# Two PSUM tiles for the transposes of attention's weights, and products in the order of the blocks

## The chip, the cores and the metric

The kernel runs on one core of a Trainium2 chip. The metric is the device time of one execution in microseconds. Three runs of the kernel before took 2699.07, 2689.06 and 2688.96 us, with a median of 2689.06 us.

## The reference

The reference is a backbone of two layers over 512 latent tokens and 256 context tokens. Each layer projects its input into four token mixers: a bidirectional RWKV-7 scan (A), a convolution module (B), windowed grouped-query attention with a sink logit (C) and multi-head latent attention, MLA (D). Their outputs are gated, projected and summed, and an output projection adds them to the stream. The change touches C and D, where softmax weights meet the values:

```
# C, per block of 128 queries and kv head (4 query heads share one kv head)
o = (jnp.einsum('bnhgqk,bnkhd->bnqhgd', (e_lat * inv).astype(v.dtype), vb)
     + jnp.einsum('bnhgqc,bchd->bnqhgd', (e_ctx * inv).astype(v.dtype), v_c))
# D, per head
p = jax.nn.softmax(s, axis=-1).astype(v.dtype)
return jnp.einsum('bhqk,bkhd->bqhd', p, v)
```

## The kernel before

All activations lie with channels on partitions. Projections are made of matmuls of 128 x 128 weights and 512 or 256 tokens. Each is done three times over on split operands (high by high, high by low, low by high; lines 289 to 291, in `mm3`), and `dense` sums them in a PSUM tile named `d`.

A layer runs in stages: RWKV, then `window` (C), then `mla` (D), then `merge`. The program is written in that order, but a scheduler lays each engine's instructions out ahead of time. It fills TensorE's places in `window` and `mla` with products of `merge` that are ready: gate projections (`hxh`, `hxl`) and branch projections (`uh`, `ul`). These are called fillers below. What is not used up as a filler runs in `merge` itself. Every engine works through its list strictly in order, so a place in the list is fixed before the run.

Attention works in units. A unit of `window` is a block of 128 queries with one kv head, thus four query heads; it has 4 or 5 blocks of 128 keys, or 2 for context queries. A unit of `mla` is one head with all its queries: 6 blocks of keys and 512 queries in the latent part, and 2 blocks and 256 queries in the context part, which layer 0 alone has. For each row of a unit TensorE makes scores in a PSUM tile `S`, VectorE takes the maximum (L1019), ScalarE the exponential (L1025), and VectorE normalises (L1032). The weights lie in an SBUF tile `P` (named `aP` in `window`, `mP` in `mla`) with queries on partitions.

`weighted_values` (L1041) then turns them round. For each block of keys, TensorE transposes the 4 (or 2) pieces of 128 x 128 into the PSUM tile `T` (L1050). `pt_copy` copies `T` back over `P`, by turns on ScalarE (L1037) and VectorE (L1039). Then a matmul for each block multiplies with the values (L1054) and sums in the PSUM tile `E`. A block with an even number writes partitions 0 to 63 of `E`, one with an odd number partitions 64 to 127, so that each half of `E` has its own sum. `halves` (L1060, L1061) adds the two and so empties `E`. Both pools hold one tile: the transposes of a block wait until the copy of the block before is done. The products run from the last block to the first, so that the first product waits for the copy that is made last.

Inside `weighted_values`, TensorE's transposes and products keep the written order among themselves (`manual_schedule`), while the scheduler may still put other work between any two of them. The readout of a unit is placed behind the scores of the next. `T` also serves `conv_norm` and, in layer 0, `ada_later`, which makes the modulation of the next layer in small steps (L379, L389) from weights that come by DMA. Nothing else uses `E` in these two stages.

Of the kernel before, what the change touches and what calls it, by code (L numbers as in the profile page):

```python
# [215 lines left out]
class Net:  # L216
# [821 lines left out]
        else:  # L1038
            self.nc.vector.tensor_copy(out, in_)  # L1039

    def weighted_values(self, P, values, acc):  # L1041


        nc = self.nc
        nk, nb = P.shape[1:3]
        with self.tc.manual_schedule(engines={mybir.EngineType.PE}):
            for x in range(nk):
                pt = self.pT([128, nb, 128])
                for i in range(nb):
                    nc.tensor.transpose(pt[:, i], P[:, x, i], self.c("ident"))  # L1050
                self.pt_copy(P[:, x], pt)
            for n, x in enumerate(reversed(range(nk))):
                half = slice(64 * (x % 2), 64 * (x % 2) + 64)
                nc.tensor.matmul(acc[half], lhsT=values(x), rhs=P[:, x].rearrange("p i q -> p (i q)"),  # L1054
                                 start=n < 2, stop=n >= nk - 2)

    def halves(self, pool, out, acc, tag):

# [60 lines left out]
    def window(self, l, ap, nxt):  # L1119
# [8 lines left out]
        vt = ap.tile([128, 6, 128], F32, tag="avt", name=self.n("avt"), bufs=1)  # L1128
# [7 lines left out]
        for kv in range(2):  # L1136
            rows = slice(64 * kv, 64 * kv + 64)
# [30 lines left out]

        def readout(P, kblocks, kv, st, dst):
            rows = slice(64 * kv, 64 * kv + 64)  # L1170
            acc = self.pE([128, 512])
            self.weighted_values(P, lambda x: vt[:, kblocks[x], rows], acc)
            for _ in range(ASTEP * len(kblocks)):
                next(ada, None)
            self.halves(ap, st[rows].rearrange("p a b -> p (a b)"), acc, "aOh")
            if kv:
                nc.sync.dma_start(dst, st)

        for seg in full[::-1]:
            s0, s1 = seg  # L1180
            lat = s0 > 0
            qs = self.aq if lat else self.window_queries(s0, s1)
            nb = (s1 - s0) // 128
            for b in range(nb):
                lo, hi = (max(0, b - 1), min(nb, b + 2)) if lat else (0, 0)
                kblocks = [0, 1] + [2 + kb for kb in range(lo, hi)]
                nk = len(kblocks)
                st = ap.tile([128, 4, 128], F32, tag="aO", name=self.n("aO"), bufs=2)
                for kv in range(2):
                    P = ap.tile([128, 5, 4, 128], F32, tag="aP", name=self.n("aP"), bufs=2)[:, :nk]  # L1190
                    qt = stack(qs[:, :, 128 * b:128 * b + 128], kv)
                    self.softmax(ap, [(lambda i=i: scores(qt[:, 128 * i:128 * i + 128], kv, b, lo, hi, nb, lat),
                                       P[:, :, i]) for i in range(4)], WA_SCALE,
                                 (self.pm("sink", 4 * kv, 4), sk8[:, 4 * kv:4 * kv + 4]))
                    units += 1
                    if units >= CONV_AT:
                        next(conv, None)
                    if pending:
                        readout(*pending.pop())
                    pending.append((P, kblocks, kv, st, self.y[2][:, :, s0 + 128 * b:s0 + 128 * b + 128]))  # L1200
        readout(*pending.pop())
        for rest in (conv, ada):
            for _ in rest:
# [12 lines left out]
    def mla(self, l, ap):  # L1216
# [39 lines left out]
        for s0, s1 in both:  # L1256
            x = ck[:, s0:s1]
# [4 lines left out]
        vt = ap.tile([128, 6, 512], F32, tag="mvt", name=self.n("mvt"), bufs=1)  # L1262
# [21 lines left out]
        def readout(P, h, s0, s1):  # L1284
            n = s1 - s0
            rows = slice(64 * (h % 2), 64 * (h % 2) + 64)
            acc = self.pE([128, n])
            self.weighted_values(P, lambda kb: vt[:, kb, 64 * h:64 * h + 64], acc)
            st = ap.tile([128, n], F32, tag="mO", name=self.n("mO"), bufs=1)
            self.halves(ap, st[rows], acc, "mOh")  # L1290
            nc.sync.dma_start(self.y[3][rows, h // 2, s0:s1], st[rows])

        for s0, s1 in full[::-1]:
            n = s1 - s0
            lat = s0 > 0
            nb = n // 128
            ksegs = both if lat else (SEG_C,)
            nk = 6 if lat else 2
            qn = [self.hilo(ap, x, f"mq{i}") for i, x in enumerate(normed(
                [load(f"dq{i}", s0, s1, f"mq{'hl'[i]}") for i in range(2)], "qn"))]  # L1300
            for hp in range(4):
# [3 lines left out]
                for hh in range(2):  # L1305
                    h = 2 * hp + hh
# [30 lines left out]
                    P = ap.tile([128, 6, 4, 128], F32, tag="mP", name=self.n("mP"), bufs=2)  # L1337
                    P = P.rearrange("p k i q -> p (k i q)")[:, :nk * n].rearrange("p (k i q) -> p k i q", i=nb, q=128)
                    for b in range(nb):
                        self.softmax(ap, [(lambda: scores(b), P[:, :, b])], MLA_SCALE)  # L1340
                        if b == nb - 2 and pending:
                            readout(*pending.pop())
                    pending.append((P, h, s0, s1))
        readout(*pending.pop())


# [215 lines left out]
```

## Time and profile before

| | |
|---|---|
| median of three runs | 2689.06 us |
| the profiled execution | 2689.9 us |
| its span, from first to last instruction | 2688.1 us |
| TensorE matmul busy | 2498.9 us (93% of the span) |
| VectorE busy | 1900.9 us (71%) |
| ScalarE busy | 1294.8 us (48%) |
| GpSimd busy | 612.1 us (23%) |

In the profile PE is TensorE's matmuls, PEld its weight loads, DVE VectorE and ACT ScalarE. L1050 is a line of the kernel. The recorded end of a matmul is modelled and overlaps the next one. What a matmul costs TensorE is therefore read from its start to the start of the next, not from its duration. A product in plain float32 (L1054) is two matmul records, so that "x12" on that line is six products. In the profiled execution `window` lies at 805 to 1001 us in layer 0 and at 2203 to 2334 us in layer 1, and the units of `mla` at 1117 to 1325 us and at 2400 to 2554 us.

### The profile page before, as it was taken

The page shows a single profiled execution, that of the slowest core. Times are in us where ns is not written, and L with a number is a line of the kernel's source. Part 1 is how long each engine was busy: PE and PEld are TensorE (multiplying, and loading weights), DVE is VectorE, ACT ScalarE, POOL GpSimd, SP SyncE. Part 2 cuts the span into 40 slices and gives each one's busy share as a digit, 9 for nine tenths or more (in the row PEclk, how much of TensorE's full clock was granted, in tenths as well). Part 3 has the DMA queues.
Part 4 walks back from the last instruction along what each step waited for, and adds up shares of the span by engine and source line. Part 5 has one row for each costly group of instructions (what it writes and reads, how often), then busy time and mean ns, then how long its engine had stood idle before and what let it go on. Part 6 is the DMA issues. An engine that isn't in the chain of part 4 may idle for free. (4 is left out here: it accounts for less than half of the span.)

```text
span 2688.1 us, 48510 instructions
## 1 busy us (share of the span) xinstructions
PE 2498.9 (93%) x18622; PEld 1918.6 (71%) x18622; DVE 1900.9 (71%) x3644; ACT 1294.8 (48%) x2723; POOL 612.1 (23%) x644
## 2 busy tenths in 40 slices
PE   7989899898998998999999998897989899999998
PEld 5777777676886676776788876676667666666677
DVE  5788989987527564677633678887777947577835
ACT  5625474554334453445422463554565346555434
POOL 1232222222220111100132013322232421221140
PEclk9999989998999999999999999898999989999999
DMA  6321222223243346112322532223232432331233
GB/s 235 120 91 51 87 73 92 75 77 105 93 136 103 114 141 194 52 36 66 96 81 83 179 105 94 92 72 112 66 108 65 129 109 75 110 102 34 88 123 122
DMA packets 171031, 267.79 MB, mean 100 GB/s; under 512 B 18480, under 2 KB 69552, under 8 KB 170800
## 3 DMA queue, kind: packets, MB, share of 16 engines
q1 hardware_dynamic: 169520, 263.12, 31.1%
q8 instruction: 146, 2.39, 0.4%
q10 hardware_dynamic: 1280, 1.57, 0.2%
q14 instruction: 85, 0.70, 0.1%
HBM read 209.70 MB, written 54.92 MB: 98 GB/s over the span
## 5 line engine op out<-in xcount | busy, mean ns | idle before, releaser
L283 POOL TENSOR_TENSOR wl<-raw,wh 128x512 fp32r<-128x512 f32 x374 | 511.0, 1367 | 1513.1 <-ACT wh L282 1311.1
L289 PE MATMUL d<-hxh,wh 128*128 128x512 f32 (+1 forms) x1936 | 718.0, 371 | 22.8 <-DVE stg L927 12.6
L290 PE MATMUL d<-hxl,wh 128*128 128x512 f32 (+1 forms) x1936 | 717.7, 371 | 0.0
L291 PE MATMUL d<-hxh,wl 128*128 128x512 f32 (+1 forms) x1936 | 713.1, 368 | 0.0
L282 ACT CAST wh<-raw 128x512 fp32r<-128x512 f32 x420 | 259.4, 619 | 518.7 <-PE d L290 339.8
L289 PEld LDWEIGHTS d<-hxh,wh 128*128 128x128 f32 x1936 | 374.3, 193 | 78.2 <-DVE stg L927 10.3
L291 PEld LDWEIGHTS d<-hxh,wl 128*128 128x128 f32 x1936 | 374.1, 193 | 52.2 <-issue 1.6
L290 PEld LDWEIGHTS d<-hxl,wh 128*128 128x128 f32 x1936 | 375.0, 194 | 50.6 <-issue 1.8
L971 DVE SCALAR_TENSOR_TENSOR cacc<-cu,par,cacc 128x512 f32<-128x512 f32 (+1 forms) x360 | 282.0, 783 | 4.0
L289 PE MATMUL d<-uh,wh 128*128 128x512 f32 (+1 forms) x384 | 141.5, 371 | 10.7 <-ACT gt L1376 5.8
L1019 DVE TENSOR_REDUCE st<-S 128x1 f32<-128x768 f32 (+3 forms) x160 | 119.7, 763 | 33.4 <-PE S L1165 15.3
L290 PE MATMUL d<-ul,wh 128*128 128x512 f32 (+1 forms) x384 | 140.5, 367 | 0.2 <-DVE ul L1368 0.2
L291 PE MATMUL d<-uh,wl 128*128 128x512 f32 (+1 forms) x384 | 139.8, 365 | 0.0
L1383 DVE SCALAR_TENSOR_TENSOR gt<-gt,d 128x256 f32<-128x256 f32 (+1 forms) x72 | 42.8, 595 | 126.2 <-PE d L291 124.2
L721 DVE TENSOR_TENSOR Xt<-B,X 128x31 f32<-128x31 f32 (+15 forms) x248 | 107.1, 432 | 5.4 <-POOL X L716 2.0
L723 DVE TENSOR_TENSOR X<-X,Xt 128x31 f32<-128x31 f32 (+15 forms) x248 | 101.3, 409 | 3.1
L1025 ACT ACTIVATE mP<-S,st 128x768 f32<-128x768 f32 (+1 forms) x80 | 65.0, 814 | 68.8 <-DVE st L1021 64.1
L711 ACT COPY AT<-G 32x128 f32<-32x128 f32 x192 | 79.3, 413 | 26.7 <-DVE G L693 24.2
L289 PEld LDWEIGHTS d<-uh,wh 128*128 128x128 f32 x384 | 73.2, 191 | 24.5 <-ACT gt L1376 7.3
L688 PE MATMUL A<-KR,KB 64*128 64x128 f32 (+1 forms) x768 | 79.8, 292 | 7.5 <-DVE G L693 5.3
L843 POOL TENSOR_TENSOR MD<-M,Dl 128x128 f32<-128x128 f32 x80 | 42.4, 529 | 181.2 <-DVE M L845 157.9
L290 PEld LDWEIGHTS d<-ul,wh 128*128 128x128 f32 x384 | 73.3, 191 | 11.3 <-DVE ul L1368 1.5
(325 smaller groups left out, 4830.9 us busy)
## 6 DMA issues: line engine op xcount, KB each, us to landing
raw<-in_w_in SPq DMA_DIRECT2D x316, 256.0 KB, 2.7
raw<-in_w_br SPq DMA_DIRECT2D x64, 256.0 KB, 2.7
ada<-in_ada_slim SPq DMA_DIRECT2D x64, 256.0 KB, 3.3
raw<-in_w_out SPq DMA_DIRECT2D x40, 256.0 KB, 2.8
ada<-in_ada SPq DMA_DIRECT2D x32, 256.0 KB, 5.2
spz<-stg SPq DMA_DIRECT2D x32, 256.0 KB, 2.3
kvx<-wa SPq DMA_DIRECT2D x24, 256.0 KB, 3.4
yl<-y SPq DMA_DIRECT2D x16, 384.0 KB, 3.6
```

Of the source, the lines that this page charges most:

```text
L282: nc.scalar.copy(hi, raw)
L283: self.low_engine.tensor_tensor(out=lo, in0=raw, in1=hi.bitcast(F32), op=ALU.subtract)
L289: mm(ps, lhsT=wh, rhs=xh, start=first, stop=False)
L290: mm(ps, lhsT=wh, rhs=xl, start=False, stop=False)
L291: mm(ps, lhsT=wl, rhs=xh, start=False, stop=last)
L688: nc.tensor.matmul(pss[j][:, i, d, :w], lhsT=KB[rows, d, cl + i].rearrange("p a b -> p (a b)"), rhs=KR[rows, cl + i, 0:w // 64, d, :], sta ...
L711: S.copy(AT[b, :, 4 * x:4 * x + 4].rearrange("p t q -> p q t"), G.rearrange("p j i d t -> p (j i) d t")[b, :, d, 32 * h:32 * h + 32])
L721: V.tensor_tensor(out=tv, in0=B[:, t, 0:t].unsqueeze(2).to_broadcast([128, t, w]), in1=X[:, t:t + 1, t:32].to_broadcast([128, t, w]), op=A ...
L723: V.tensor_tensor(out=X[:, 0:t, t:32], in0=X[:, 0:t, t:32], in1=tv, op=ALU.subtract)
L971: V.scalar_tensor_tensor(out=acc, in0=u[:, k:n + k], scalar=w, in1=acc, op0=ALU.mult, op1=ALU.add)
L1019: V.tensor_reduce(out=m[:, i:i + 1], in_=ps, axis=AX.X, op=ALU.max)
L1025: S.activation(P, ps.rearrange("p (k c) -> p k c", c=128), AF.Exp, bias=nm[:, i:i + 1], scale=scale, accum_out=tot[:, i:i + 1])
```

## The change

`weighted_values` makes its own accumulator and returns it. The transposes of a block go to `T` or to a tile of the pool `E` by turns, so that the last block is always in `T` and the one before it in `E`. The accumulator is the next tile of `E`, so that it waits for the copy of the last block but one. The products run from the first block to the last.

```
-    def weighted_values(self, P, values, acc):
+    def weighted_values(self, P, values):
...
             for x in range(nk):
-                pt = self.pT([128, nb, 128])
+                pt = (self.pT if (nk - x) % 2 else self.pE)([128, nb, 128])
                 for i in range(nb):
                     nc.tensor.transpose(pt[:, i], P[:, x, i], self.c("ident"))
                 self.pt_copy(P[:, x], pt)
-            for n, x in enumerate(reversed(range(nk))):
+            acc = self.pE([128, nb * 128])
+            for x in range(nk):
                 half = slice(64 * (x % 2), 64 * (x % 2) + 64)
                 nc.tensor.matmul(acc[half], lhsT=values(x), rhs=P[:, x].rearrange("p i q -> p (i q)"),
-                                 start=n < 2, stop=n >= nk - 2)
+                                 start=x < 2, stop=x >= nk - 2)
+        return acc
...
         def readout(P, kblocks, kv, st, dst):
             rows = slice(64 * kv, 64 * kv + 64)
-            acc = self.pE([128, 512])
-            self.weighted_values(P, lambda x: vt[:, kblocks[x], rows], acc)
+            acc = self.weighted_values(P, lambda x: vt[:, kblocks[x], rows])
...
         def readout(P, h, s0, s1):
             n = s1 - s0
             rows = slice(64 * (h % 2), 64 * (h % 2) + 64)
-            acc = self.pE([128, n])
-            self.weighted_values(P, lambda kb: vt[:, kb, 64 * h:64 * h + 64], acc)
+            acc = self.weighted_values(P, lambda kb: vt[:, kb, 64 * h:64 * h + 64])
```

In the changed kernel the transposes stand on L1051 and the products on L1056; other lines below them move by 3 at most. The scheduler lays out every engine's list anew, and it moves instructions at two kinds of places on TensorE.

The first place is the first unit of `window` with 5 blocks in layer 0, on TensorE. `T` and `E` are the PSUM tiles, `aP` the weights, `avt` the values, `d` a filler, `S` scores. Before, with the first block, the last two and the products:

```order
L1050 MATMUL T_9363<-cst,aP_9130 128x128 x4
L290 MATMUL d_12770<-hxl_405,wh_12765 128x256
...
L1050 MATMUL T_9381<-cst,aP_9130 128x128 x4
L289 MATMUL d_12795<-hxh_402,wh_12759 128x512
L290 MATMUL d_12795<-hxl_403,wh_12759 128x512
L291 MATMUL d_12795<-hxh_402,wl_12760 128x512
L289 MATMUL d_12795<-hxh_404,wh_12765 128x512
L1050 MATMUL T_9387<-cst,aP_9130 128x128 x4
L290 MATMUL d_12795<-hxl_405,wh_12765 128x512
L291 MATMUL d_12795<-hxh_404,wl_12766 128x512
L289 MATMUL d_12795<-hxh_406,wh_12765 128x512
L290 MATMUL d_12795<-hxl_407,wh_12765 128x512
L1054 MATMUL E_9360<-aP_9130,avt_8913 64x512 x5
```

The same unit in the changed kernel, whole:

```order
L1051 MATMUL T_9362<-cst,aP_9130 128x128 x4
L1051 MATMUL E_9368<-cst,aP_9130 128x128 x4
L1051 MATMUL T_9374<-cst,aP_9130 128x128 x4
L1163 MATMUL S_9486<-akh_7822,aqs_9469 128x256
L1164 MATMUL S_9486<-akl_8924,aqs_9469 128x256
L1163 MATMUL S_9486<-akh_7822,aqs_9469 128x384
L1051 MATMUL E_9380<-cst,aP_9130 128x128 x4
L1164 MATMUL S_9486<-akl_8924,aqs_9469 128x384
...
L1051 MATMUL T_9386<-cst,aP_9130 128x128 x4
L1056 MATMUL E_9392<-aP_9130,avt_8913 64x512 x5
```

The fillers between the blocks have moved out of the unit; the five products still stand together, directly behind the last transposes.

The second place is the third latent unit of `mla` in layer 0, on TensorE; `mP` are its weights, `mvt` the values, `ck` and `mku` the operands of the keys' projection for the next head. Before:

```order
L289 MATMUL d_14077<-uh_13480,wh_14059 128x512
L290 MATMUL d_14077<-ul_13481,wh_14059 128x512
L291 MATMUL d_14077<-uh_13480,wl_14060 128x512
L1054 MATMUL E_11470<-mP_11305,mvt_10994 64x512 x6
L1312 MATMUL S_11542<-ck_10969,mku_11540 64x512
```

The same unit in the changed kernel:

```order
L1051 MATMUL T_11502<-cst,mP_11305 128x128 x4
L1056 MATMUL E_11508<-mP_11305,mvt_10994 64x512 x5
L289 MATMUL S_11458<-mKh_11031,mqh_11426 128x512
L290 MATMUL S_11458<-mKl_11032,mqh_11426 128x512
L291 MATMUL S_11458<-mKh_11031,mql_11427 128x512
L289 MATMUL S_11458<-mKh_11031,mqh_11426 128x256
L290 MATMUL S_11458<-mKl_11032,mqh_11426 128x256
L291 MATMUL S_11458<-mKh_11031,mql_11427 128x256
L1056 MATMUL E_11508<-mP_11305,mvt_10994 64x512
L289 MATMUL S_11522<-mKh_11031,mqh_11426 128x512
```

Six products in one group have become a group of five, six score matmuls, and one product by itself. The same happens in 14 of the 16 latent units of `mla`; a fifteenth goes from groups of 4 and 2 to groups of 3, 2 and 1. In 7 of the 8 context units, and in 2 of the 4 context units of `window`, a group of two becomes two products apart.

## Rows read from the trace of the kernel before

**Rows 1.** Busy time by stretch: length, then PE, PEld, DVE, ACT, POOL, PEclk, DMA.
```profile
805.00:1001.00 196.00, 182.93 (x1601) 132.60 (x1599) 131.49 (x308) 98.45 (x225) 23.84 (x18) 0.97 0.39 117
1117.00:1325.00 208.00, 204.77 (x1132) 145.29 (x1131) 156.97 (x321) 107.11 (x233) 24.25 (x18) 1.00 0.18 50
2203.00:2334.00 131.00, 118.27 (x623) 81.71 (x622) 95.55 (x190) 73.91 (x152) 25.04 (x18) 0.96 0.26 81
2400.00:2554.00 154.00, 149.72 (x750) 100.90 (x748) 123.53 (x220) 75.03 (x143) 25.55 (x19) 1.00 0.21 61
```

**Rows 2.** TensorE's waits, 805 to 1001 us: total us, times, longest.
```profile
PE T L1050 <- DVE aP L1039: 2.5, 2, 2.1
...
PE E L1054 <- DVE aP L1039: 1.4, 1, 1.4
...
PE E L1054 <- ACT aP L1037: 0.7, 1, 0.7
```

**Rows 3.** TensorE's waits, 2203 to 2334 us.
```profile
PE E L1054 <- DVE aP L1039: 2.0, 2, 1.4
...
PE T L1050 <- ACT aP L1037: 1.6, 1, 1.6
PE T L1050 <- DVE aP L1039: 1.3, 2, 0.8
```

**Rows 4.** TensorE's waits, 2400 to 2554 us.
```profile
PE T L1050 <- ACT mP L1037: 0.7, 1, 0.7
```

**Rows 5.** Timeline, layer 1's `window`: start us, us, engine, line, operation [idle before].
```profile
2318.25 0.60 PE L1050 MATMUL T<-cst,aP 128*128 128x128 f32 x4
2318.93 0.68 DVE L1039 COPY aP<-T 128x512 f32<-128x512 f32 x1
...
2319.66 0.66 PE L1050 MATMUL T<-cst,aP 128*128 128x128 f32 x4 [0.81 <-DVE aP L1039]
```

**Rows 6.** Timeline of TensorE around six products, layer 1's `mla`.
```profile
2531.71 0.28 PE L290 MATMUL S<-mKl,mqh 96*128 96x256 f32 x1
2531.83 0.28 PE L291 MATMUL S<-mKh,mql 96*128 96x256 f32 x1
2532.04 2.79 PE L1054 MATMUL E<-mP,mvt 128*64 128x512 f32 x12
2534.77 0.50 PE L289 MATMUL S<-mKh,mqh 96*128 96x512 f32 x1
2535.10 0.39 PE L290 MATMUL S<-mKl,mqh 96*128 96x512 f32 x1
2535.34 0.39 PE L291 MATMUL S<-mKh,mql 96*128 96x512 f32 x1
```

**Rows 7.** The same around five products, layer 0's `window`.
```profile
874.26 2.79 PE L1054 MATMUL E<-aP,avt 128*64 128x512 f32 x10
876.98 0.61 PE L389 MATMUL T<-cst,adas 128*128 128x2 f32 x4
```

**Rows 8.** The same around four products and two products, layer 0's `mla`.
```profile
1264.40 1.94 PE L1054 MATMUL E<-mP,mvt 128*64 128x512 f32 x8
1266.27 0.39 PE L289 MATMUL S<-mq0h,mwh 128*128 128x256 f32 x1
...
1267.18 1.08 PE L1054 MATMUL E<-mP,mvt 128*64 128x512 f32 x4
1268.20 0.39 PE L289 MATMUL S<-mKh,mqh 96*128 96x256 f32 x1
```

**Rows 9.** The same around six products that the keys' projection follows, layer 0's `mla`.
```profile
1173.02 2.80 PE L1054 MATMUL E<-mP,mvt 128*64 128x512 f32 x12
1175.65 1.45 PE L1312 MATMUL S<-ck,mku 128*64 128x512 f32 x4
```

**Rows 10.** The same around a context unit's two products of 256 queries, layer 0's `mla`.
```profile
1290.87 0.65 PE L1054 MATMUL E<-mP,mvt 128*64 128x256 f32 x4
1291.45 0.39 PE L289 MATMUL d<-hxh,wh 128*128 128x256 f32 x1
```

## The prediction

> **What bounds the kernel now.** I read the busy times by stretch first. In the stretches of the attention units TensorE is recorded busy for 182.93 of 196 us, 204.77 of 208, 118.27 of 131 and 149.72 of 154 us [rows 1]. It idles there 13.1, 3.2, 12.7 and 4.3 us, 33.3 us in all. VectorE, the next, is busy for 131.49, 156.97, 95.55 and 123.53 us [rows 1]: much used, but not the bound. So TensorE's list sets the pace. It is filled up with the merge's products, and a filler that is not done here is done in the merge. Two things therefore move the end: idle time of TensorE in these stretches, and work that is added to its list.
>
> Then I read TensorE's waits, for those that the one tile `T` causes, that is waits for a copy. In layer 0's `window` they are 2.5, 1.4 and 0.7 us [rows 2], in layer 1's 2.0, 1.6 and 1.3 us [rows 3], and in layer 1's `mla` 0.7 us stands out [rows 4]. Together 10.2 us. That is all that the second tile can give back directly.
>
> Last I read the timeline around the products, from start to start. Two, four and six products take 1.02, 1.87 and 2.73 us [rows 8, 6]: 0.15 us and then 0.86 us for each pair. Five take 2.72 us [rows 7], as long as six. So two products that write different halves of `E` run side by side, and one without a partner costs as much as two. That is what this change must be judged by.
>
> **The second tile.** Transposes, copies and products are as many as before: 192 blocks in 44 units. A block returned to the tile of the block before it 148 times (192 less 44); now a block returns to the tile of the one before that, 104 times (192 less 88). How long such a return takes can be seen where nothing covers it: the four transposes start at 2318.25, the copy runs from 2318.93 to 2319.61, and the next transposes start at 2319.66, after 0.81 us of waiting [rows 5]. In the changed order the four transposes of the block between two uses of a tile cover up to 0.60 us of that [rows 5], and fewer fillers stand between the blocks. Some places have nothing else (the third block of the first unit shown), most have score matmuls or fillers. So most of the 10.2 us should go, not all. Ends: 0 if copies are late because of what stands ahead of them on ScalarE and VectorE, 10.2 us if every such wait goes. A loss is among the rivals. I take 9 us, near the upper end, because the wait of rows 5 is of the kind that the other tile covers, and it is where six of the seven waits lie, in `window`.
>
> None of the transposes is added or taken away, so I cost their new places at nothing. The move of accumulator and transposes into one pool adds a wait too: a unit's first transposes may need the `E` that `halves` of the unit before has yet to empty. Between the products of one unit and the transposes of the next stands the softmax of a whole unit, so I cost this at nothing too. Without that cover, a copy and an addition of some 1.3 us (twice the copy of rows 5) would show at each unit.
>
> The rule of the Trainium skill that speaks against this term is in "TensorE: Matmul & The Clock Gate", section "HAM oscillation — how this bites in real kernels": after a kernel's order was mended, double-buffering PSUM gave no further gain. By that rule the 9 us are 0 and the sum below rises by as much. It is one kernel's experience and not this one's; rows 5 shows a wait that another tile would have covered.
>
> **The order of the products.** Going backwards, the first product waited for the last copy, and then nothing held the others: the scheduler left six in one group. Going forwards, only the last product waits for the last copy, and the scheduler puts six score matmuls ahead of it. A group of six becomes a group of five and one alone. The five cost 2.72 us, so nothing is saved, and the single one is paid on top. Its price: two products alone in a group take 1.02 us, and one without a partner takes the same. A group also lengthens the step of the matmul ahead of it, from 0.12 to 0.21 us, and of the one behind, from 0.24 to 0.33 us [rows 6]. So 1.02 + 0.09 + 0.09 = 1.2 us for a group. 15 latent units of `mla` are split: 15 x 1.2 = 18.0 us. In 12 of these 15 the keys' projection, of the same shape, stood right behind the group, and the six took only 2.63 us [rows 9]. There the group loses 0.10 us more, its successor is lengthened by 0.09, and the projection gets a step of 0.09 of its own: 12 x 0.28 = 3.4 us. In 7 context units of `mla` a pair of 0.58 us [rows 10] becomes two groups: 7 x (0.58 + 0.18) = 5.3 us. In `window` 2 context units are split: 2.4 us. Together 29 us. The low end counts the passes alone, 17 x 0.86 + 7 x 0.43 = 17.6 us; I take 29, since rows 6 and 8 show the switches.
>
> All of it is on TensorE's list in stretches where it is busy for 98% (204.77 of 208) and 97% (149.72 of 154) of the time [rows 1], so nothing hides it: fillers are pushed into the merge by as much.
>
> **What else moves.** The scheduler lays out ScalarE, VectorE and the DMA queue anew, with the same instructions; the loads of the merge's operands move later along with their fillers. GpSimd's list keeps its order. I cost this at nothing: TensorE's own work covers it. Without that cover the price is more idle time in `window`; it belongs to the third rival.
>
> **Sum.** Against the profiled execution of 2689.9 us: + 29 - 9 = + 20, thus 2709.9. The median of the runs is 0.8 us lower than that execution, so **2709 us**. With both terms at their ends, this case spans + 7 to + 29, thus 2696 to 2718.
>
> **Rivals.**
>
> *The idle time pays for it.* With transposes early, ScalarE and VectorE get their copies early, and softmax runs ahead of TensorE. If the idle time of both `window` stretches goes, 13.1 + 12.7 = 25.8 us [rows 1], the sum is 29 - 25.8 = + 3: 2692 us. For it: the waits for copies are only part of that idle time. Against it: the rest are waits for softmax itself, whose work is not less, and there are fewer fillers to bridge them.
>
> *The single product hides (faster).* Half of the array is free beside it. If a neighbouring score matmul could run there as a partner does, the 29 us would be 0 and only gains would be left, between 10.2 us (the copies) and 33.3 us (all idle time of these stretches); midway 2667 us. It decides if over 13.4 us come back. Against it: the fifth product of rows 7 has neighbours and still costs the full 0.85 us over four, and the step behind a group is longer, not shorter [rows 6].
>
> *The second tile gives nothing back.* Copies stand in ScalarE's and VectorE's lists among softmax work, and fewer fillers bridge each delay. Then the waits stay and the sum is + 29: 2718 us. If they double, another 10.2 us come on top: 2728 us. For it: VectorE is busy for 73% of layer 1's `window` (95.55 of 131) [rows 1], so its copies are often late. The rule of the Trainium skill cited above ("TensorE: Matmul & The Clock Gate") amounts to this outcome.
>
> *The change does not do what it says.* The order excludes that for the tiles. For "products begin with the first block" it shows the split that the forecast rests on.
>
> **How the numbers follow.** About 0.5%, 13.4 us, is what a measurement of this kernel can tell from no change; so faster is below 2675.6 and slower above 2702.5. The forecast gets 0.52: its price per group is read from four kinds of groups. Of that I put 0.08 below 2702.5 and 0.44 above. The idle time that pays gets 0.25, all within 0.5%. The hidden product gets 0.07. No gain from the tile gets 0.16, all above. So slower 0.60, same 0.33, faster 0.07. The range 2690 to 2730 us holds the forecast, nearly all of the third rival and some 0.15 of the first, 0.80 in all.
>
> **What would show it.** Right: "x10" and "x2" records of the products in `mla` where "x12" stood, the single one about 1 us before its successor; a step of TensorE in `mla`, from unit to unit, that holds less filler; waits for copies below 5 us in all; and a merge that begins with more products left. Wrong: single products below 0.5 us to their successor, or idle time in `window` that falls by 20 us or more (the forecast is then too high), or that grows (too low).

## The result, and the profile after

The changed kernel took 2731.41 us, a median of four runs (2729.23 to 2736.11); beside it the kernel before took 2689.01 us. The ratio is 1.0156, with a 95% interval of 1.0129 to 1.0183: slower by 42 us, where + 20 us was forecast. The end of the range was 2730. The profiled execution took 2729.53 us.

First the page's row of TensorE in the changed kernel:

```profile
PE 2535.0 (93%) x18622; PEld 1931.3 (71%) x18622; DVE 1909.9 (70%) x3644; ACT 1297.6 (48%) x2725; POOL 611.6 (22%) x644
```

It is busy for 36.1 us more than the 2498.9 us before, with as many instructions, so part of it is a price in time for the same work. Next the busy time by stage. The six stretches are `window`, `mla` and `merge` of layer 0 and of layer 1, cut at the first transposes of weights, the last products of `window`, the last products of `mla` and the first load of the next layer. Columns: stretch, length, then PE, PEld, DVE, ACT, POOL, PEclk, DMA. The kernel before:

```profile
808.70:1001.50 192.80, 180.84 (x1587) 131.05 (x1587) 127.85 (x298) 96.90 (x220) 23.84 (x18) 0.97 0.39 117
1001.50:1323.40 321.90, 308.50 (x1986) 226.58 (x1982) 211.94 (x403) 150.55 (x309) 45.09 (x34) 0.99 0.28 84
1323.40:1569.80 246.40, 242.44 (x1369) 210.50 (x1366) 119.72 (x165) 82.75 (x145) 48.03 (x43) 1.00 0.37 117
2218.10:2332.90 114.80, 106.24 (x568) 72.36 (x566) 83.18 (x165) 66.33 (x134) 23.53 (x17) 0.99 0.25 76
2332.90:2553.40 220.50, 209.65 (x998) 144.98 (x994) 166.20 (x270) 110.72 (x200) 47.52 (x35) 1.00 0.29 85
2553.40:2688.10 134.70, 121.53 (x611) 102.11 (x607) 64.14 (x88) 49.75 (x91) 32.98 (x27) 0.96 0.38 122
```

The changed kernel:

```profile
804.60:971.00 166.40, 156.79 (x1442) 109.58 (x1443) 124.04 (x294) 90.70 (x210) 15.76 (x12) 0.98 0.43 127
971.00:1284.30 313.30, 302.07 (x1870) 212.00 (x1867) 198.14 (x388) 143.80 (x298) 40.38 (x30) 0.99 0.26 75
1284.30:1584.70 300.40, 290.89 (x1627) 251.47 (x1625) 138.58 (x184) 95.16 (x166) 61.05 (x53) 0.98 0.36 112
2237.00:2330.10 93.10, 86.56 (x485) 58.86 (x484) 83.34 (x162) 61.18 (x125) 14.82 (x11) 0.98 0.22 68
2330.10:2552.40 222.30, 211.07 (x948) 140.73 (x946) 153.78 (x250) 109.08 (x194) 41.19 (x31) 0.98 0.23 69
2552.40:2727.70 175.30, 154.85 (x742) 127.44 (x738) 83.14 (x111) 59.80 (x108) 47.54 (x38) 0.94 0.41 127
```

The attention stages became shorter, by 54.9 us in all (850.0 to 795.1), and hold fewer instructions of TensorE. The merges became longer, by 94.6 us (381.1 to 475.7). The six stretches together grew from 1231.1 to 1270.8 us, + 39.7; all other stages together stayed the same within 0.2 us. Five parts make up the 39.7 us:

| us, in the six stretches | before | after | difference |
|---|---|---|---|
| TensorE idle in attention (length less busy) | 44.8 | 38.6 | - 6.2 |
| TensorE idle in the merges | 17.1 | 30.0 | + 12.8 |
| half clock in attention | 10.2 | 11.9 | + 1.7 |
| half clock in the merges | 4.9 | 14.9 | + 10.0 |
| busy, less half clock | 1154.0 | 1175.4 | + 21.4 |

"Half clock" is half the length of the stretches in which the trace has a granted clock of 0.50, the lower of the engine's two levels (1.2 of 2.4 GHz): the time that the lower clock adds, if TensorE has work throughout. The rounded PEclk column agrees. The last row is the price of the other order of the products. The forecast had it, and the returned waits; it had nothing for the merges' idle time and clock, 22.8 us.

Now the products, in TensorE's timeline of one latent unit of `mla` in the changed kernel:

```profile
1096.78 0.38 PE L1051 MATMUL T<-cst,mP 128*128 128x128 f32 x2
1097.09 2.79 PE L1056 MATMUL E<-mP,mvt 128*64 128x512 f32 x10
1099.81 0.50 PE L289 MATMUL S<-mKh,mqh 96*128 96x512 f32 x1
...
1100.84 0.28 PE L291 MATMUL S<-mKh,mql 96*128 96x256 f32 x1
1101.05 1.07 PE L1056 MATMUL E<-mP,mvt 128*64 128x512 f32 x2
1102.05 0.50 PE L289 MATMUL S<-mKh,mqh 96*128 96x512 f32 x1
1102.39 0.40 PE L290 MATMUL S<-mKl,mqh 96*128 96x512 f32 x1
```

From start to start, five products take 2.72 us, as six did [rows 6], and the single one takes 1.00 us, as a pair did [rows 8]. The matmul ahead of the single one takes 0.21 us instead of 0.12, the one behind it 0.34 instead of 0.24. In the whole trace there are 14 such groups of ten records, and 15 single products of 512 queries in `mla`.

TensorE's waits for copies, and one for `halves`, in the changed kernel: the first line is of layer 0's `window`, the next three of layer 1's, the last of layer 1's `mla` (us in all, times, longest):

```profile
PE T L1051 <- DVE aP L1039: 2.5, 3, 2.0
...
PE E L1056 <- ACT aP L1037: 1.4, 1, 1.4
...
PE E L1056 <- DVE aP L1039: 0.6, 1, 0.6
PE E L1051 <- DVE aO L1064: 0.4, 1, 0.4
...
PE T L1051 <- DVE mP L1039: 0.2, 1, 0.2
```

The copies cost 4.7 us where those of before cost 10.2 [rows 2 to 4]. The new wait, for the addition of `halves` (on `aO`), costs 0.4 us.

Last, the merge. The waits of the products of gated operands (`uh`, `ul`), in the whole program: busy, mean ns, then idle time before them and what ended it. The kernel before:

```profile
L289 PE MATMUL d<-uh,wh 128*128 128x512 f32 (+1 forms) x384 | 141.5, 371 | 10.7 <-ACT gt L1376 5.8 <-ACT uh L1367 4.9
```

The changed kernel:

```profile
L289 PE MATMUL d<-uh,wh 128*128 128x512 f32 (+1 forms) x384 | 142.2, 376 | 24.1 <-ACT uh L1368 18.9 <-DVE gt L1384 2.5 <-ACT gt L1377 2.5
```

The wait for `uh` grew from 4.9 to 18.9 us. `uh` is the high part of a branch's gated output. For each of its four tiles `merge` loads the output (`yl`) and a gate (`zt`), VectorE multiplies them (L1365 of the changed kernel), ScalarE makes `uh` (L1368) and VectorE `ul` (L1369). The branches come in the order A, B, C, D. Those of A, B and C use a pool with one buffer of `yl`, one of `zt` and four of `uh`, so C's operands can only be made when B's last products have read theirs, and one tile after another. When were they made? ScalarE's instructions that write `uh`, of branches C and D, first and last start: in the kernel before, in layer 0 and in layer 1:

```profile
L1367 ACT CAST uh<-zt x8: 832/834/842, 1255.4 to 1346.1; 128x768 fp32r<-128x768 f32 x8
...
L1367 ACT CAST uh<-zt x8: 617/620/632, 2503.2 to 2573.0; 128x512 fp32r<-128x512 f32 x8
```

In the changed kernel:

```profile
L1368 ACT CAST uh<-zt x8: 831/835/837, 1296.3 to 1321.3; 128x768 fp32r<-128x768 f32 x8
...
L1368 ACT CAST uh<-zt x8: 607/618/621, 2563.4 to 2583.0; 128x512 fp32r<-128x512 f32 x8
```

Before, C's operands were begun at 1255.4 and 2503.2 us, 68 and 50 us ahead of the end of `mla` (1323.4 and 2553.4). In the changed kernel they come at 1296.3 and 2563.4 us, 12 and 11 us behind it (1284.3 and 2552.4), and the operands of both C and D, eight tiles, are made in 20 to 25 us at the start of the merge. What that looks like in the changed kernel, on all engines:

```profile
1312.53 0.39 PE L291 MATMUL d<-uh,wl 128*128 128x512 f32 x1
1314.06 0.96 DVE L1365 TENSOR_TENSOR zt<-zt,yl 128x768 f32<-128x768 f32 x1 [3.37 <-DMA zt<-spz]
...
1315.05 0.83 ACT L1368 CAST uh<-zt 128x768 fp32r<-128x768 f32 x1 [3.82 <-DVE zt L1365]
...
1315.93 1.01 PE L289 MATMUL d<-uh,wh 128*128 128x256 f32 x2 [3.01 <-ACT uh L1368]
```

The load comes in, VectorE and ScalarE take 0.96 and 0.83 us, and TensorE has waited for 3.01 us. At about the same time its clock falls. Busy times and PEclk in two stretches of the merges of the changed kernel:

```profile
1315.52:1325.72 10.20, 6.18 (x18) 4.09 (x19) 4.12 (x6) 1.81 (x3) 0.55 (x1) 0.50 0.26 77
2571.66:2581.80 10.14, 5.79 (x12) 3.56 (x12) 4.07 (x6) 1.85 (x3) 0.00 (x0) 0.50 0.56 172
```

The granted clock is 0.50 in both. Each stretch costs some 5 us beside the waits in it. In the kernel before, the whole merge of layer 0 was granted 1.00.

### The profile page after: what moved, and what is told of

Its sections match the earlier page's. It is cut to its first block, busy times and chain, and to the rows that moved or that the text cites. A ratio compares the mean times of both kernels' runs of the same rounds, so it can differ in the third digit from the quotient of the medians.

```text
span 2727.7 us, 48559 instructions
## 1 busy us (share of the span) xinstructions
PE 2535.0 (93%) x18622; PEld 1931.3 (71%) x18622; DVE 1909.9 (70%) x3644; ACT 1297.6 (48%) x2725; POOL 611.6 (22%) x644
## 5 line engine op out<-in xcount | busy, mean ns | idle before, releaser
L289 PE MATMUL d<-hxh,wh 128*128 128x512 f32 (+1 forms) x1936 | 716.2, 370 | 21.4 <-DVE stg L927 13.7
L289 PEld LDWEIGHTS d<-hxh,wh 128*128 128x128 f32 x1936 | 373.9, 193 | 78.0 <-DVE stg L927 10.2
L289 PE MATMUL d<-uh,wh 128*128 128x512 f32 (+1 forms) x384 | 142.2, 376 | 24.1 <-ACT uh L1368 18.9
L1025 ACT ACTIVATE mP<-S,st 128x768 f32<-128x768 f32 (+1 forms) x80 | 64.8, 814 | 68.0 <-DVE st L1021 67.1
```

The costliest lines, as they stand in the source:

```text
L289: mm(ps, lhsT=wh, rhs=xh, start=first, stop=False)
L1025: S.activation(P, ps.rearrange("p (k c) -> p k c", c=128), AF.Exp, bias=nm[:, i:i + 1], scale=scale, accum_out=tot[:, i:i + 1])
```

## The experiments

**Theory A**: the loss has two parts, the split products, and the third branch's operands. The latter, which fillers used to cover in attention, are prepared in the open when the merge begins, which costs idle time and clock. **Theory B**, the rival: the split products alone, at a higher price than forecast, and scatter.

The first four runs take the change apart. *Two tiles, products backwards* keeps the second tile and undoes the order (against the changed kernel):

```
-            for x in range(nk):
+            for n, x in enumerate(reversed(range(nk))):
...
-                                 start=x < 2, stop=x >= nk - 2)
+                                 start=n < 2, stop=n >= nk - 2)
```

> Two tiles as in the change, but the products run from the last block to the first as before. Theory A (the loss is the split products, 29 us, and the fillers that leave attention, whose inputs are then prepared in the open at the start of the merge): no product stands alone; 12 latent units of mla get one group more (4 and 2), 0.33 us each or 4 us; 6 us of waits come back; but in the order the third branch's first products stand behind the last product of mla, so the merge idles about 12 us more than before, with up to 10 us at half clock: 2695 to 2705 us. Theory B (the split alone, the rest scatter): 2689 + 4 - 9 = 2684 us and no new idle time in the merge.

*One tile, products forwards* is the opposite (the lines with a minus put into the kernel before).

> One tile as before, but the products run from the first block to the last. Here 8 context pairs, 2 latent groups of mla and 2 groups of window are split: 8 x 0.76 + 4 x 1.2 = 11 us. The third branch's products stand within attention as before, so theories A and B both expect about 2700 us; A also expects the idle time of the two merges as before (4 and 13 us).

*Last pair swapped* is the changed kernel with another order of the products, so that the last block comes ahead of the one before it and the last two products wait together:

```
+            for n, x in enumerate([*range(nk - 2), nk - 1, nk - 2]):
```

> The change with the last two products exchanged, so that both wait for the last copy and nothing divides the pair. Theory A: some 26 us of lone products go, the open preparation at the merge stays, since the third branch stands behind mla in the order: 2698 to 2708 us, with about 12 us more idle time in the merges than before. Theory B: 2683 us.

*Window alone* leaves `mla` with one tile and products backwards:

```
-            acc = self.weighted_values(P, lambda kb: vt[:, kb, 64 * h:64 * h + 64])
+            acc = self.weighted_values(P, lambda kb: vt[:, kb, 64 * h:64 * h + 64], self.pE([128, n]))
```

> The change in window alone; mla keeps one tile and products backwards. Two pairs are split (2.4 us). Theory A: the waits of window come back in part (5 us), but the third branch stands behind mla in the order, so the merge idles some 10 us more, with some half clock: 2692 to 2705 us. Theory B: 2689 + 2 - 5 = 2686 us.

All results stand in one table. Idle time and half clock are those of both merges; "uh" is TensorE's wait for `uh` in the row shown above; "busy" is busy time less half clock in the six stretches.

| kernel | median us | ratio to before, 95% | idle | half clock | uh | busy |
|---|---|---|---|---|---|---|
| before | 2689 to 2693 | 1 | 17.1 | 4.9 | 4.9 | 1154.0 |
| changed | 2731.41 | 1.0156 (1.0129 to 1.0183) | 30.0 | 14.9 | 18.9 | 1175.4 |
| two tiles, backwards | 2710.31 | 1.0069 (1.0042 to 1.0096) | 25.3 | 11.1 | 9.9 | 1154.3 |
| one tile, forwards | 2705.29 | 1.0051 (1.0034 to 1.0068) | 19.1 | 7.3 | 7.1 | 1173.5 |
| last pair swapped | 2706.56 | 1.0055 (1.0031 to 1.0078) | 30.1 | 17.6 | 18.9 | 1151.1 |
| window alone | 2706.27 | 1.0057 (1.0036 to 1.0077) | 29.0 | 11.8 | 19.8 | 1153.0 |
| changed, gates of the second | 2717.62 | 1.0099 (1.0077 to 1.0121) | 14.5 | 3.1 | 7.0 | 1175.7 |
| before, gates of the second | 2697.39 | 1.0025 (1.0005 to 1.0044) | 13.5 | 3.7 | 8.9 | 1151.0 |
| last pair swapped, gates of the second | 2692.53 | 0.9999 (0.9981 to 1.0017) | 13.7 | 2.7 | 5.5 | 1153.5 |
| window alone, gates of the second | 2696.11 | 1.0007 (0.9989 to 1.0026) | 14.8 | 3.0 | 6.3 | 1153.9 |
| one tile, last pair swapped | 2691.30 | 0.9987 (0.9971 to 1.0004) | 19.0 | 7.0 | 5.5 | 1159.1 |
| before, two branches' operands | 2684.74 | 0.9976 (0.9960 to 0.9992) | 16.5 | 7.4 | 4.4 | 1150.6 |
| changed, two branches' operands | 2706.58 | 1.0058 (1.0035 to 1.0080) | 14.8 | 3.2 | 5.8 | 1175.0 |

What the first four say: where the order of blocks is kept forwards to the end (changed kernel; one tile, forwards), the column "busy" is some 20 us higher; in all others it is as before. So the order has a price of its own, with one tile too. It is not the split alone: "one tile, forwards" leaves a single product in two latent units of `mla`, the changed kernel in 15, and its column is still 19.5 us higher, against 11 us expected. It took 5 us more than the 2700 us of its expectation. But the three kernels with the second tile whose pairs stay together (in "window alone" all but two pairs of context units) are slower too, by 15 to 19 us, with no more busy time on TensorE. That speaks against B, whose 2683 to 2686 us missed by 20 us and more. They lose it in the merges. The row of "last pair swapped" shows it as the changed kernel's did:

```profile
L289 PE MATMUL d<-uh,wh 128*128 128x512 f32 (+1 forms) x384 | 141.0, 373 | 24.1 <-ACT uh L1368 18.9 <-ACT gt L1377 3.7 <-DVE gt L1384 1.4
```

"Two tiles, backwards" came out 5 us above what A allowed. In its profile the stages outside the six stretches are 14 us longer than before, though nothing was changed in them, and its uh wait is the smallest of the three. How much of its 19 us the merges cost is thus less sure than in the other two. "Window alone" came out 1 us above what A allowed.

The next four move the cover back, with no change to attention. Some gate projections are made early in each layer, those of the third branch (3 in layer 0, 8 in layer 1). Making the second branch's early instead leaves B less to do, so that C's operands come into `mla` again, and leaves C's gate projections as work that needs none of these operands. One line, put into the changed kernel, into the kernel before, into "last pair swapped" and into "window alone":

```
-AHEAD = tuple([(2, 7 - i) for i in range(n)] for n in (3, 8))
+AHEAD = tuple([(1, 7 - i) for i in range(n)] for n in (3, 8))
```

> The change, but the gate projections that are made ahead of attention (3 in layer 0, 8 in layer 1) belong to the second branch instead of the third. The amount of work is the same. The second branch is then done earlier, so the third branch's first products stand ahead of the end of mla in the order, and its inputs are prepared under attention. Theory A (lone products, plus open preparation at the merge): the lone products stay (23 us), the merges' idle time falls back to about 17 us in both together from 30, and the half clock that followed it in part: 2705 to 2715 us. Theory B (the lone products and scatter alone make the 40 us): unchanged, 2725 to 2735 us.

> The kernel before with the same exchange of the gates made ahead. There the third branch stands within attention already. Both theories: within 0.3% of before, 2683 to 2699 us. If it is faster by more, the exchange is a gain of its own and has to be taken off the run before.

> The change with the last two products exchanged (pairs stay together) and with the gates of the second branch made ahead (no open preparation). Theory A: both costs are gone and the waits for copies that came back (6 us) are left: 2680 to 2692 us. Theory B: the exchange of gates does nothing, so as the run with the pair swapped, about 2706 us.

> The change in window alone, mla as before, with the gates of the second branch made ahead. Theory A: 2680 to 2694 us, as no latent unit is split and nothing is prepared in the open. Theory B: as the run with window alone, about 2706 us.

All four merges fell to 14 or 15 us of idle time and 3 or 4 us of half clock, and the three kernels with the second tile gained 10 to 14 us. B had expected no gain. "Last pair swapped" fell to the time of the kernel before, with C's first `uh` at 1243.8 us, 49 us ahead of the end of its `mla` (1292.7 us). It ended half a microsecond above what A allowed, the changed kernel and "window alone" 2 to 3 us above it. The cover is not free: in the changed kernel the merges shed 15.5 us of idle time and 11.8 us of half clock, but its attention stages took 7.3 us of idle time (38.6 to 45.9) and 6.9 us of half clock (11.9 to 18.8) more. The kernel before became 5 us slower by the line; in its profile half clock in the attention stages rose from 10.2 to 18.4 us. Measured from that kernel, "last pair swapped" is 5 us faster (2692.53 against 2697.39, with intervals that overlap), and the changed kernel 20 us slower (2717.62 against 2697.39). The row of the changed kernel with that line:

```profile
L289 PE MATMUL d<-uh,wh 128*128 128x512 f32 (+1 forms) x384 | 141.6, 373 | 10.1 <-ACT uh L1368 7.0 <-ACT gt L1377 2.6 <-DVE m L1384 0.3
```

The last three. *One tile, last pair swapped* asks what the order costs if pairs stay together and the tiles are left alone (the kernel before with the loop of "last pair swapped").

> The kernel before, with one tile for the transposes, but the products in the order of the blocks with the last two exchanged: the last product still waits for the last copy but one, the one ahead of it for the last. Most latent groups of mla stay whole (13 of 16 are x12 in the order), and the third branch's gated operands stand ahead of the last product of mla, as in the kernel before. Theory A (split products, and operands prepared in the open at the merge): neither is paid, so 2684 to 2697 us, the merges' idle time in all below 20 us. Theory B (the split alone, and scatter): the same, 2684 to 2697 us. The run does not tell A from B; it tells whether the order of the products by itself costs anything when pairs stay together, and whether it beats the kernel before.

It took as long as the kernel before. *Two branches' operands* asks the question from the other side: the third branch's operands are not made at all, and its products read the second's. That leaves out part of the computation: the loads, the gating and the splits of branch C.

```
-            us = []
-            for i in range(4):
+            us = us if n == 2 else []
+            for i in range(4 if n != 2 else 0):
```

> The kernel before, with the third branch's gated operands left out: its products read the second branch's, so its loads (zt, yl), its gating and its splits are not made. Both theories: some 2675 to 2690 us, for the few us of idle time at the merges that its operands cause. Idle time of the merges in all 10 to 16 us.

> The changed kernel with the third branch's gated operands left out in the same way. Theory A: what the merges lost went with these operands, so the gap to the other kernel that leaves them out is the split less the returned waits, +12 to +24 us, and the merges idle and run at half clock within 8 us of that kernel's. Theory B: the operands have no part in it, the gap stays at some +40 us as between the two whole kernels, and the merges idle about 30 us.

Without these operands the kernel before loses 6 us of its time and the changed kernel 25 us (2706.58 against 2731.41, measured beside two sets of runs of before that differ by 2 us). The gap between the two falls from 42 to 22 us (0.0082 of the time before, with some 0.0028, thus 7 or 8 us, of uncertainty from the two intervals). That is A's + 12 to + 24, and not B's + 40. The changed kernel's waits for `uh`, without them:

```profile
L289 PE MATMUL d<-uh,wh 128*128 128x512 f32 (+1 forms) x384 | 140.4, 369 | 9.6 <-ACT uh L1368 5.8 <-ACT gt L1377 2.5 <-DVE gt L1384 1.1
```

So some 20 of the 42 us go with the third branch's operands. No kernel that computes everything beats the kernel before by more than can be measured; the nearest, one tile with the last pair swapped, has 1 inside its interval. What would cure the cause directly, a second buffer of `yl` and `zt` or more of `uh`, was not tried.

## Why the prediction was right in direction and wrong in size

**What bounds the kernel: right.** TensorE's list sets the pace; time that it idles and work that is added to it show at the end, and fillers pushed out of attention were done in the merges, which grew by 94.6 us.

**The order of the products: right in kind, 29 us against 21 to 25.** Products forwards cost 21.4 us of busy time at full clock in the changed kernel, 24.7 between the two kernels with the gates of the second, and 24.4 between the two without the third branch's operands. The price of one group, 1.2 us, holds: 1.00 + 0.09 + 0.10. Adding up, for both traces and the six stretches, the steps from start to start less idle time and half clock gives where the rest lies: the steps of products grew by 23.3 us, those of scores by 3.2 and of transposes by 4.5, 31.0 together, near the 29 forecast. But those of the products summed in `d`, the fillers and the merge's own, shrank by 10.9 us, with as many of them. These stand behind a matmul of another kind 282 times instead of 342, now that more of them run in one piece in the merge, and the first of three with 512 columns takes 0.31 us there against 0.23 us behind one of their own. That is a step that the sum left out. It also had nothing for the transposes: with one tile and products forwards, theirs grew by 6.7 us and those of products by 13.7, while those in `d`, of which attention held 1903 (1883 before, 1493 in the changed kernel), shrank by 2.3 only.

**The second tile: right in the waits that go, wrong in what that gives back.** Waits for copies fell from the 10.2 us of the rows to 4.7, below the 5 us of the text, and the wait that pooling adds came to 0.4 us, where nothing was forecast. (The "seven waits" of the text are seven rows, with ten waits.) TensorE's idle time in attention fell by 6.2 us, but the tile alone cannot be credited with it, since the third branch's operands left these stages too. Leaving them out of the kernel before lowers that idle time by as much, from 44.8 to 38.2 us, with one tile. Attention of layer 0 and of layer 1, without these operands, in the kernel before:

```profile
814.90:1320.50 505.60, 484.36 (x3540) 351.65 (x3541) 327.67 (x692) 244.33 (x524) 67.01 (x51) 0.98 0.31 91
2221.50:2550.50 329.00, 312.02 (x1547) 214.64 (x1546) 240.29 (x422) 173.76 (x328) 67.21 (x50) 0.99 0.26 75
```

In the changed kernel:

```profile
806.80:1287.60 480.80, 460.78 (x3311) 323.20 (x3310) 321.41 (x681) 234.38 (x508) 56.19 (x42) 0.98 0.31 90
2226.70:2542.30 315.60, 297.65 (x1432) 199.30 (x1430) 236.52 (x411) 170.32 (x319) 56.61 (x41) 0.98 0.23 66
```

Length less PE is 38.2 us with one tile and 38.0 us with two. The waits for copies in these stretches fell from 9.4 to 4.7 us, and others grew: those for `uh` from 2.2 to 5.1 us, those of score matmuls for the exponential (L1025, on `aP`) from 2.9 to 5.2 us. Of layer 0's part (us in all, times, longest), in the kernel before:

```profile
PE T L1050 <- DVE aP L1039: 2.4, 2, 2.0
...
PE d L289 <- ACT uh L1367: 1.5, 2, 1.1
...
PE S L1160 <- ACT aP L1025: 1.0, 2, 0.7
```

In the changed kernel:

```profile
PE d L289 <- ACT uh L1368: 4.7, 2, 4.3
...
PE T L1051 <- DVE aP L1039: 2.5, 3, 2.0
PE S L1163 <- ACT aP L1025: 2.2, 4, 1.4
```

With the gates of the second branch it is the same: 44.9 us in the kernel before, 45.9 in the changed kernel, 44.3 in "last pair swapped". So the 5 us by which that last one is faster do not show as idle time, and its interval overlaps the other's. The forecast took a wait that goes to be time that comes back; here the time went to other waits. The rule of the Trainium skill in "TensorE: Matmul & The Clock Gate", section "HAM oscillation — how this bites in real kernels", that double-buffering PSUM gave no further gain, fits the outcome: no kernel with two tiles is measurably faster than the one before.

That the gap without the operands, 22 us, lies so near the + 20 of the forecast is thus partly luck: the price of the order was 24.4 us there and not 29, and the idle time that the tile gave back 0.2 us and not 9.

**The step that failed** is "What else moves": "the loads of the merge's operands move later along with their fillers … I cost this at nothing: TensorE's own work covers it." The cover was gone. With it fell "fillers are pushed into the merge by as much", which took a filler to cost the same in either place. In attention it bridges waits and gives a chain of load, VectorE, ScalarE and VectorE the time to run; in the merge that chain is what TensorE waits for. Its price in the merges was 12.8 us of idle time and 10.0 us of half clock; over the whole kernel, some 20 us go with these operands. The text did name the price of a lost cover, as idle time in `window`; it came in the merge, where the prediction read no row.

**The rivals.** The idle time of `window` did not pay for the split: in the two `window` stages it fell by some 4 us (from 12.0 and 8.6 to 9.6 and 6.5), where the rival had 25.8. The single product did not hide: 1.00 us each. "The second tile gives nothing back" was nearest in time, at 2718 to 2728 us. Its waits for copies did not stay, but its outcome did, as the idle time without the operands shows. It had nothing for the merge either. And the change did do what it says.

**The signs.** "x10" and "x2" appeared, the single one 1.0 us before its successor; the attention stages hold less filler; the copies' waits are below 5 us; and the merges begin with more products left. All came as written. None of them could have told of the 22.8 us, since the signs stopped where the merge begins.

**What stays open.** The tile alone cost 19 or 15 us and the order alone 14 us, 29 to 33 together, where both cost 42. The order alone does not push C's operands later: in "one tile, forwards" they are begun 74 us ahead of the end of `mla` in both layers. What makes the last 9 to 13 us, when both come together, no run shows.

## What to carry to other kernels

A wait that goes is not yet time that comes back: look at the stage's whole idle time too. And work that fills a stage's gaps does two things: it uses the gaps, and it moves the preparation of what comes next ahead of time. Before making such a stage shorter, look up when the operands of the next stage are made, how many buffers they have, and what would cover them if the fillers were done later. And where two matmuls run side by side in the array, an order that lets one of them go early takes its partner away: here the early one saved nothing (five products took 2.72 us, six 2.73), and the late one cost as much as a pair (1.00 against 1.02 us).

## What was not expected of the hardware

In the merges of the changed kernel, waits of 2 to 4 us came with some 10 us at the lower clock in each merge, though TensorE had been busy for most of the time before:

```profile
1303.00:1315.50 12.50, 9.41 (x45) 7.24 (x44) 8.61 (x9) 5.14 (x9) 4.79 (x3) 1.00 0.70 202
2562.00:2571.60 9.60, 6.33 (x26) 4.29 (x24) 7.63 (x9) 3.90 (x7) 3.37 (x3) 1.00 0.74 246
```

These are the stretches just ahead of the two at 0.50. TensorE was busy for 9.41 of 12.50 us and 6.33 of 9.60 us in them, at full clock. So the merges' 12.8 us of added idle time came with 10.0 us of added half clock, and cost nearly twice what the idle time says. The clock is also a source of scatter: the half clock in the first 700 us, which no edit but the one of the gates touches, varied from 27 to 44 us between the profiles of the other kernels.
